# A decoder layer's last experts: four finished late, weights in megabytes, sums loaded through GpSimd's queue

## The chip, the cores and the metric

The kernel runs on one core of a Trainium2 chip. The metric is the time of one execution on the device in microseconds (us), the median of several runs. TensorE does the matrix products, VectorE and ScalarE the element-wise work, GpSimd a few small operations and the gathers and scatters by index; SyncE issues most transfers. Sixteen DMA engines move the data of all queues.

## What is computed

One decoder layer on 1024 tokens of width 1024 in float32: a chunked recurrence and a sliding-window attention, gated and mixed, then a LayerNorm, then a mixture of 32 experts (each token goes to one group of eight and there to two experts), then a second LayerNorm. Only the experts and the second LayerNorm matter here:

```python
def expert_block(args):
    xb, e = args
    h = jax.nn.silu(xb @ w_gate[e]) * (xb @ w_up[e])
    return h @ w_down[e]
...
    y = jnp.zeros((T, D), x.dtype).at[slot_tok].add(ybuf * slot_w[:, None].astype(x.dtype))
...
x = layer_norm(DN_ALPHA * x + moe, ln2_g[l], ln2_b[l])
```

An expert's weights are 1024x512 twice and 512x1024 once, 6 MB.

## The kernel before

The first tokens of an expert are gathered at 760 us; from there the experts run one after the other, in the order of `ORDER`, with the experts of `LAST` at the end. An expert's number below is its place in that order, 0 to 31. Its tokens are gathered by index on GpSimd (xg), turned by TensorE, and multiplied.

*Splits.* A float32 matrix is used as a sum of two parts: `split` casts a rounded part on ScalarE (eh, L98) and subtracts it on VectorE (el, L99), and `mm3` makes three products of the parts (L103 to L105). The weights from expert 31's gate on (and down of 30 and 31, which come later) are used unsplit, as float32 straight from the fetched tile er (L1187).

*Pieces.* `first_pieces` lists the weights in 384 pieces of 512 KB in the order of use: gate and up of expert e+1 (eight pieces), then down of e (four). `fetch` issues a piece's load on SyncE, at most DEEP = 8 under way. `moe` goes through the pieces: `halve` asks for the split of the piece LA = 3 ahead, then the steps that are due are written (results, sums), then the products of the piece, then a fetch. The order in which each engine gets its instructions here is the order in which this loop writes them.

*Results.* A normal expert's result is scaled on ScalarE and added to the sums zd in device memory by an indirect transfer of GpSimd (`accumulate`, L1090). The late experts (LAST has one of each of three groups, so no token goes to two of them) leave zd alone: their rows of zd are gathered (zf, L1086), `finish` adds the result (L1362), the LayerNorm follows in place, and the finished rows are written by index to the output (L1365). For all other tokens `final` plans the loads of zd in eight tiles z on SyncE (L1309), a sum on ScalarE (L1318), and `norm2`: mean (fm), squares on ScalarE (L1342), rsqrt (fv, on VectorE and GpSimd, L700 and L701), a gain and a shift on VectorE (L1346, L1349), and the store on SyncE (L1322). The indexed writes wait for all eight stores, since they write over some of their rows.

*Memory.* Raw pieces, both parts of a split, z, zf and scratch share 36 slots of 4 KB per partition (tag q4); a new tile waits until its slot's last user is done.

Of the kernel before, what the change touches and what calls it, by code (L numbers as in the profile page):

```python
# [23 lines left out]
LAST = (15, 23, 31)  # L24
# [37 lines left out]
class Builder:  # L62
# [5 lines left out]

    S2 = {"ob", "as", "aph", "apl", "ach", "acl", "oT", "hq", "hk", "hl", "hv", "hg", "hkd", "hkT", "hqb", "hst", "hE", "hS", "hsq", "ho",
          "rxT", "rlT", "hh", "hth", "htl"}  # L70
    NQ = 36
    NX = 9
    NRAW = 29
    LA = 3

    def __init__(self, tc, aps):
        self.tc, self.nc, self.a = tc, tc.nc, aps

    def tile(self, shape, dt, tag, bufs, name=None):
        name = name or tag  # L80
        if tag in self.S2:
            tag, bufs = "s2", self.n2
        pool = self.base if tag in ("q4", "st2", "base") else self.sb
# [78 lines left out]
    def load_x(self, half, j):  # L162
        raw = self.q4([128, 2, 512], name="xr")
        self.nc.sync.dma_start(raw, self.a["xt"][half, j])
        return raw

    def split_x(self, half, raws):

        self.xh.append([])
        self.xl.append([])  # L170
        for raw in raws:
            h, l = self.q4([128, 2, 512], F32R, "xh"), self.q4([128, 2, 512], F32R, "xl")
# [12 lines left out]
    def wload_half(self, c0, q):  # L185
        raw = self.q4([128, 4, 256], name=f"wr{c0}")
        self.nc.sync.dma_start(raw, self.a["w_in"][c0 // 256, q])
        return raw
# [4 lines left out]
    def wsplit_half(self, raw):  # L193
        h = self.q4([128, 4, 256], F32R, "wh")
        l = self.q4([128, 4, 256], F32R, "wl")
        self.split(h, l, raw)
        return h, l
# [45 lines left out]
    def att_proj(self):  # L243
# [11 lines left out]
        self.aq = [self.q4([128, 4, 256], name=f"aq{i}") for i in range(4)]  # L255
# [32 lines left out]
        self.ak = self.q4([128, T], name="ak")  # L288
# [231 lines left out]
    def hgrn(self):  # L520
# [83 lines left out]
        def prep_levels(n, hs):  # L604
            t = self.q4([128, 2, 512], F32, "hE")
# [98 lines left out]
    def mixing_loads(self):  # L704

        nc = self.nc
        self.stages, self.late_stages = {}, {}
        self.wab, self.ot, self.gates = {}, {}, {}
        wv = [self.a[nm].rearrange("(k p) c -> p k c", p=128) for nm in ("w_a", "w_b")]

        def load_wab(jt, when):
            raw = self.q4([128, 2, 4, 128], name="wab")
            for i in range(2):
                nc.sync.dma_start(raw[:, i], wv[i][:, :, jt * 128:jt * 128 + 128])
            self.at(2 * when, lambda: self.halves(self.wab, jt, raw), True)

        def load_o(b, half, nm, j):
            raw = self.q4([128, 2, 512], name=f"o{nm}")
            d = self.obd if nm == "b" else self.oad
            nc.sync.dma_start(raw, d.rearrange("k p t -> p k t")[:, 2 * j:2 * j + 2, half * 512:half * 512 + 512])  # L720
# [15 lines left out]
    def halves(self, dst, key, raw, eng=None):  # L736
        h, l = self.q4(raw.shape, F32R, "h"), self.q4(raw.shape, F32R, "l")
        self.split(h, l, raw, eng)
        dst[key] = h, l
# [23 lines left out]
    def mixing(self):  # L763
# [27 lines left out]
        def load_wo(b, p):  # L791
            raw = self.q4([128, 2, 512], name="wo")
            c, kp = p // 4, p % 4
            nc.sync.dma_start(raw, wov[:, 2 * kp:2 * kp + 2, c * 512:c * 512 + 512])
            self.at(2 * b + 2, lambda: halves(wo, p, raw, nc.gpsimd))
# [5 lines left out]
        def branch(half, jt):  # L801
# [10 lines left out]
            if jt % 2 == 0:  # L812
                mg[jt // 2] = self.q4([128, 2, 512], F32R, "mh"), self.q4([128, 2, 512], F32R, "ml")
# [71 lines left out]
        for b in range(24, 31):  # L885
            for _ in range(2 if b % 2 else 1):
                at(before, b, lambda b: self.fetch())
# [3 lines left out]
        while tick < 2 * len(main) or stages or self.late_stages:  # L891
# [19 lines left out]
            if tick >= 2 * len(main) - 1:  # L911
                for _ in range(4 if tick < 2 * len(main) + 1 else 2):
                    self.fetch(True)
# [179 lines left out]
    def first_pieces(self):  # L1093
# [14 lines left out]
        self.first_whole = self.pieces.index((NE - 1, "w_g", 0))  # L1108
        self.raws, self.fetched = {}, []

    def whole(self, e, m):

        return self.pieces.index((e, m, 0)) >= self.first_whole

    def fetch(self, first=False):

        n = len(self.fetched)
        if n >= len(self.pieces) or first and n >= self.NRAW:
            return
        e, m, k = self.pieces[n]  # L1120
        x = ORDER[e]
        if m == "w_d":
            r = self.q4([128, 1, D], name="er")
            ins = self.nc.sync.dma_start(r, self.a[m][x].rearrange("(k p) c -> p k c", p=128)[:, k:k + 1])
        else:
            r = self.q4([128, 2, 512], name="er")
            ins = self.nc.sync.dma_start(r, self.a[m][x, k])
# [115 lines left out]
    def halve(self, i):  # L1243
        if i >= len(self.pieces):
            return
        e, m, k = self.pieces[i]
        raw = self.raws.pop(i)
        if i >= self.first_whole:
            self.V["w", e, m, k] = raw, None
            return  # L1250
        h = self.q4(raw.shape, F32R, name="eh")
        l = self.q4(raw.shape, F32R, name="el")
        self.split(h, l, raw)
        self.V["w", e, m, k] = h, l

    def step(self, at, fn):

        self.steps.setdefault(int(at), []).append(fn)

    def moe(self):  # L1260
# [18 lines left out]
        self.final(at[NE - len(LAST) - 1, "w_d", 3] + 3)  # L1279
        for i in range(n):  # L1280
            self.halve(i + self.LA)
            self.now = i
            for fn in self.steps.pop(i, []):
                fn()
# [3 lines left out]
            if post:  # L1288
                self.step(i + 1 + (i < n - 4), post)
            self.fetch()  # L1290
# [6 lines left out]
    def final(self, first):  # L1297
# [9 lines left out]
        def load(i):  # L1307
            z = self.q4([128, D], name="z")
            nc.sync.dma_start(z, self.zd[i * 128:i * 128 + 128, :])  # L1309
            self.zs.append(z)  # L1310

        def rows(e):
            self.zf[e] = self.q4([128, D], name="zf")
            self.gather_rows(self.zf[e], self.zd, e)

        def sums(i):
            s = self.tile([128, 1], F32, "fs", 3)
            nc.scalar.activation(self.q4([128, D], name="w"), self.zs[i], AF.Copy, accum_out=s)  # L1318
# [6 lines left out]
        for i in range(8):  # L1325
            self.step(first + i, lambda i=i: load(i))
            self.step(first + 8 + 1.75 * i, lambda i=i: self.norm2(self.zs[i], sums(i), lambda: store(i)))
        for j in range(len(LAST)):
            self.step(first + 8 + j, lambda j=j: rows(NE - len(LAST) + j))
        self.stored = int(first + 8 + 1.75 * 7) + 4  # L1330

    def norm2(self, z, s, then):

        nc, vec = self.nc, self.nc.vector
        m, v = self.tile([128, 1], F32, "fm", 3), self.tile([128, 1], F32, "fv", 3)
# [5 lines left out]
        def square():  # L1341
            nc.scalar.activation(self.q4([128, D], name="w"), z, AF.Square, bias=m, accum_out=v)  # L1342
# [9 lines left out]
        square()  # L1352
        self.step(self.now + 1, gain)
        self.step(self.now + 2, shift)
# [47 lines left out]
    def more(self, e):  # L1402
# [16 lines left out]
        for nm in ("w_g", "w_u"):  # L1419
            ps = self.bank("mm")  # L1420
            for k in range(8):
                w = self.st2()
                nc.sync.dma_start(w, self.a[nm][bass.ds(e, 1), k // 2].rearrange("o p i c -> (o p) i c")[:, k % 2])
# [11 lines left out]
        wv = self.a["w_d"][bass.ds(e, 1)].rearrange("o (k p) c -> p (o k) c", p=128)  # L1435
        for j in range(2):
            ps = self.bank("mm")
            for k in range(4):
                w = self.st2()
                nc.sync.dma_start(w, wv[:, k, j * 512:j * 512 + 512])  # L1440
# [37 lines left out]
def gate_up(w):  # L1478

    return np.ascontiguousarray(w.reshape(NE, 4, 2, 128, 512).transpose(0, 1, 3, 2, 4))  # L1480


def arrays(inputs):
# [15 lines left out]
        "w_g": gate_up(f["w_exp_gate"][0]),  # L1499
        "w_u": gate_up(f["w_exp_up"][0]),  # L1500
        "w_d": f["w_exp_down"][0],
# [18 lines left out]
```

## Time and profile before

| | |
|---|---|
| median of 3 runs | 1399.96 us (1399.85 to 1399.97) |
| the profiled execution | 1399.95 us, its span 1398.2 us |
| TensorE busy | 1335.6 us (96%) |
| VectorE busy | 1080.5 us (77%) |
| ScalarE busy | 789.4 us (56%) |
| GpSimd busy | 241.8 us (17%) |

Busy time and span are those of the one profiled execution; 1.75 us of its time lie outside the span. In the profile's rows PE is TensorE, DVE VectorE, ACT ScalarE, POOL GpSimd, SP SyncE; a q behind the name is the engine's queue of DMA issues. Times are microseconds from the span's start, unless in ns.

### The profile page before, as it was taken

What the parts mean: (1) busy time and instruction counts of PE and PEld (TensorE: products, weight loads), DVE (VectorE), ACT (ScalarE), POOL (GpSimd) and SP (SyncE); (2) the same over time, 40 slices, a digit from 0 to 9 for tenths busy, and PEclk for the clock granted to TensorE, in tenths of its full rate; (3) what the DMA queues carried; (4) which work ended last, traced back from release to release, by engine and by line L of the source; (5) the groups of instructions that cost most, each with busy time, mean ns of one, the idle gap of its engine ahead of it and who ended that gap; (6) DMA issues with size and microseconds to landing.
All of it is one profiled execution on the core that took longest, in us unless ns stands there. A gap on an engine that the chain in (4) does not pass through costs nothing. (4 is left out here: it accounts for less than half of the span.)

```text
span 1398.2 us, 22818 instructions
## 1 busy us (share of the span) xinstructions
PE 1335.6 (96%) x8314; PEld 1100.5 (79%) x8314; DVE 1080.5 (77%) x1798; ACT 789.4 (56%) x1282; POOL 241.8 (17%) x160
## 2 busy tenths in 40 slices
PE   7999999999999999999998999999999999999844
PEld 5888899987788887788787888888888888888621
DVE  4268985779989956668656989999999999999645
ACT  4367644335545532312112888888888888888542
POOL 0001312120000002300001122222222222222123
PEclk9999999999999999999999999999999999999967
DMA  6124232153444436763557999999999999999962
GB/s 246 56 89 145 100 112 76 39 169 114 137 128 146 148 103 194 254 211 121 196 195 287 356 368 369 366 356 354 353 357 358 352 358 357 367 360 365 369 251 97
DMA packets 142564, 327.84 MB, mean 234 GB/s; under 512 B 18614, under 2 KB 59702, under 8 KB 142448
## 3 DMA queue, kind: packets, MB, share of 16 engines
q1 hardware_dynamic: 132800, 308.78, 60.9%
q0 software_dynamic: 9648, 17.57, 4.9%
q8 instruction: 66, 1.08, 0.3%
q14 instruction: 50, 0.41, 0.1%
HBM read 291.43 MB, written 52.43 MB: 246 GB/s over the span
## 5 line engine op out<-in xcount | busy, mean ns | idle before, releaser
L99 DVE TENSOR_TENSOR el<-er,eh 128x1024 fp32r<-128x1024 f32 x368 | 436.8, 1223 | 53.4 <-ACT eh L98 37.8
L98 ACT CAST eh<-er 128x1024 fp32r<-128x1024 f32 x368 | 369.7, 1054 | 99.5 <-PE mm L104 82.7
L103 PE MATMUL mm<-xh,wh 128*128 128x512 f32 x480 | 194.9, 406 | 7.8 <-ACT wh L98 6.8
L103 PE MATMUL mm<-eh,xh 128*128 128x512 f32 x496 | 196.4, 396 | 0.0
L104 PE MATMUL mm<-el,xh 128*128 128x512 f32 x496 | 196.2, 395 | 0.0
L105 PE MATMUL mm<-eh,xl 128*128 128x512 f32 x496 | 196.1, 395 | 0.0
L104 PE MATMUL mm<-xl,wh 128*128 128x512 f32 x480 | 189.0, 394 | 0.8 <-DVE xl L99 0.8
L105 PE MATMUL mm<-xh,wl 128*128 128x512 f32 x480 | 189.1, 394 | 0.0
L103 PEld LDWEIGHTS mm<-xh,wh 128*128 128x128 f32 x480 | 91.4, 190 | 25.7 <-ACT wh L98 6.8
L105 PEld LDWEIGHTS mm<-eh,xl 128*128 128x128 f32 x496 | 93.2, 188 | 22.5
L104 PEld LDWEIGHTS mm<-el,xh 128*128 128x128 f32 x496 | 93.2, 188 | 22.3
L103 PEld LDWEIGHTS mm<-eh,xh 128*128 128x128 f32 x496 | 93.2, 188 | 22.3
L105 PEld LDWEIGHTS mm<-xh,wl 128*128 128x128 f32 x480 | 91.2, 190 | 20.6 <-DVE wl L99 0.8
L1086 POOL DMA_INDIRECT xg<-x1d,gi x32 | 58.1, 1816 | 279.3 <-PE pb L1149 255.4
L104 PEld LDWEIGHTS mm<-xl,wh 128*128 128x128 f32 x480 | 91.4, 190 | 17.7 <-DVE xl L99 1.1
L103 PE MATMUL mm<-eh,hth 128*128 128x512 f32 x240 | 100.2, 418 | 0.0
L1090 POOL DMA_INDIRECT zd<-y,gi x29 | 69.8, 2407 | 156.5 <-ACT y L1240 156.5
L105 PE MATMUL mm<-eh,htl 128*128 128x512 f32 x240 | 94.8, 395 | 0.0
L104 PE MATMUL mm<-el,hth 128*128 128x512 f32 x240 | 94.8, 395 | 0.0
L103 PE MATMUL mm<-wh,xh 128*128 128x256 f32 x256 | 73.1, 286 | 0.0
L105 PE MATMUL mm<-wh,xl 128*128 128x256 f32 x256 | 72.4, 283 | 0.0
L104 PE MATMUL mm<-wl,xh 128*128 128x256 f32 x256 | 72.4, 283 | 0.0
(257 smaller groups left out, 2522.7 us busy)
## 6 DMA issues: line engine op xcount, KB each, us to landing
er<-w_g SPq DMA_DIRECT2D x128, 512.0 KB
er<-w_u SPq DMA_DIRECT2D x128, 512.0 KB
er<-w_d SPq DMA_DIRECT2D x128, 512.0 KB
wr<-w_in SPq DMA_DIRECT2D x38, 512.0 KB
gated<-st SPq DMA_DIRECT2D x32, 256.0 KB
st<-gated SPq DMA_DIRECT2D x32, 256.0 KB
xr<-xt SPq DMA_DIRECT2D x8, 512.0 KB
wab<-w_a SPq DMA_DIRECT2D x16, 256.0 KB
```

Of the source, the lines that this page charges most:

```text
L98: self.nc.scalar.copy(hi, src)
L99: (eng or self.nc.vector).tensor_sub(lo, src, hi.bitcast(F32))
L103: mm(out, lh, rh, start=start, stop=False)
L104: mm(out, lh, rl, start=False, stop=False)
L105: mm(out, ll, rh, start=False, stop=stop)
L1086: self.nc.gpsimd.indirect_dma_start(to, None, rows, bass.IndirectOffsetOnAxis(ap=self.column(self.gi, e), axis=0), bounds_check=T - 1, oob ...
L1090: self.nc.gpsimd.indirect_dma_start(self.zd, bass.IndirectOffsetOnAxis(ap=idx, axis=0), y, None, bounds_check=T - 1, oob_is_err=False, com ...
```

## The change

- Four experts are late instead of three, so 28 accumulates instead of 29, four gathers zf and four indexed writes.
- The 36 slots of 4 KB become 18 of 8 KB. A fetch loads two pieces at once, 1 MB in rows of 8 KB (the host lays the weights out so), DEEP becomes 4; the two parts of a split share a slot, and so do two z or two zf.
- The loads of z are issued by GpSimd instead of SyncE, at the steps F+3 to F+6, where F (`first`) is the last piece of expert 27; the gathers zf follow at F+7 to F+10, the sums from F+17.
- The fetches of the last eight megabytes (gate and up of 31, down of 30 and 31) are written from F+8 on.
- From F on the due steps are written ahead of `halve`, the products' own steps first. The steps of `norm2` lie further apart. Scratch moves to another pool.
- Only expert 31 is used unsplit; down of 30 is split.

```diff
-LAST = (15, 23, 31)
+LAST = (7, 15, 23, 31)
...
-    NQ = 36
+    NQ = 18
     NX = 9
-    NRAW = 29
+    NRAW = 14
     LA = 3
...
-    def q4(self, shape, dt=F32, name="q4"):
-        return self.tile(shape, dt, "q4", self.NQ, name)
+    def q8(self, shape, dt=F32, name="q8"):
+        return self.tile(shape, dt, "q8", self.NQ, name)
+
+    def q4(self, shape, pair, dt=F32):
+
+        if pair in self.pairs:
+            t = self.pairs.pop(pair)[:, 1024:2048]
+        else:
+            t = self.pairs[pair] = self.q8([128, 2048], dt, str(pair[0]))
+            t = t[:, 0:1024]
+        return self.shaped(t, shape)
...
+    def halved(self, src, eng=None):
+
+        hi, lo = self.parts(src.shape)
+        self.split(hi, lo, src, eng)
+        return hi, lo
+
+    def parts(self, shape):
+        t = self.q8([128, 2048], F32R, "hl")
+        return self.shaped(t[:, 0:1024], shape), self.shaped(t[:, 1024:2048], shape)
...
-        self.first_whole = self.pieces.index((NE - 1, "w_g", 0))
         self.raws, self.fetched = {}, []
 
     def whole(self, e, m):
 
-        return self.pieces.index((e, m, 0)) >= self.first_whole
+        return e == NE - 1
 
     def fetch(self, first=False):
 
         n = len(self.fetched)
-        if n >= len(self.pieces) or first and n >= self.NRAW:
+        if 2 * n >= len(self.pieces) or first and n >= self.NRAW:
             return
...
+        e, m, k = self.pieces[2 * n]
+        r = self.q8([128, 2, D] if m == "w_d" else [128, 4, 512], name="er")
+        ins = self.nc.sync.dma_start(r, self.a[m][ORDER[e], k // 2])
         if n >= self.DEEP:
             self.after(ins, self.fetched[n - self.DEEP])
...
-    DEEP = 8
+    DEEP = 4
...
-        h = self.q4(raw.shape, F32R, name="eh")
-        l = self.q4(raw.shape, F32R, name="el")
-        self.split(h, l, raw)
-        self.V["w", e, m, k] = h, l
...
+        raw = self.raws[i // 2]
+        n = raw.shape[1] // 2
+        raw = raw[:, n * (i % 2):n * (i % 2) + n]
+        self.V[("w",) + self.pieces[i]] = (raw, None) if self.whole(*self.pieces[i][:2]) else self.halved(raw)
...
-        self.final(at[NE - len(LAST) - 1, "w_d", 3] + 3)
+        first = at[NE - len(LAST) - 1, "w_d", 3]
+        self.late = []
+        self.final(first)
         for i in range(n):
-            self.halve(i + self.LA)
             self.now = i
-            for fn in self.steps.pop(i, []):
+            todo = [lambda: self.halve(i + self.LA)]
+            todo[i <= first and 1:0] = self.steps.pop(i, [])
+            for fn in todo:
                 fn()
             for fn in turns.pop(i, []):
                 turn(i, fn)
             post = self.piece(*self.pieces[i])
             if post:
-                self.step(i + 1 + (i < n - 4), post)
-            self.fetch()
+                self.step(i + 1 + (i < n - 4), post, i > first)
+            if i % 2:
+                for _ in range(1 if i < first + 4 else 2):
+                    if i > first + 6 or 2 * len(self.fetched) < first + 24:
+                        if len(self.fetched) + len(self.late) < (i + self.LA) // 2 + self.NQ - 1:
+                            self.fetch()
...
         def load(i):
-            z = self.q4([128, D], name="z")
-            nc.sync.dma_start(z, self.zd[i * 128:i * 128 + 128, :])
+            z = self.q4([128, D], ("z", i // 2))
+            self.late += [i] * (1 - i % 2)
+            nc.gpsimd.dma_start(z, self.zd[i * 128:i * 128 + 128, :])
             self.zs.append(z)
...
         for i in range(8):
-            self.step(first + i, lambda i=i: load(i))
-            self.step(first + 8 + 1.75 * i, lambda i=i: self.norm2(self.zs[i], sums(i), lambda: store(i)))
+            self.step(first + 3 + i // 2, lambda i=i: load(i))
+            self.step(first + 17 + 2.4 * i, lambda i=i: self.step(self.now + 1, lambda s=sums(i): self.norm2(self.zs[i], s, lambda: store(i))))
         for j in range(len(LAST)):
-            self.step(first + 8 + j, lambda j=j: rows(NE - len(LAST) + j))
-        self.stored = int(first + 8 + 1.75 * 7) + 4
+            self.step(first + 7 + j, lambda j=j: rows(NE - len(LAST) + j))
+        self.stored = int(first + 17 + 2.4 * 7) + 6
...
-        square()
-        self.step(self.now + 1, gain)
-        self.step(self.now + 2, shift)
+        for n, fn in ((1, square), (2, gain), (4, shift)):
+            self.step(self.now + n, fn)
...
-        "w_d": f["w_exp_down"][0],
+        "w_g": blocks(f["w_exp_gate"][0]),
+        "w_u": blocks(f["w_exp_up"][0]),
+        "w_d": blocks(f["w_exp_down"][0]),

```

GpSimd's instructions from the last accumulates on (xg: tokens of an expert; zd<-y: an accumulate; z: sums; zf: rows of a late expert; fv: rsqrt), before:

```order
L1090 DMA zd<-y,gi 1024x1024
L1086 DMA xg_8003<-x1d,gi 128x1024
L1090 DMA zd<-y,gi 1024x1024 x2
L1086 DMA zf<-zd,gi 128x1024 x2
L701 TENSOR_TENSOR fv<-fv,mhalf 128x1
L1086 DMA zf<-zd,gi 128x1024
L701 TENSOR_TENSOR fv<-fv,mhalf 128x1 x8
L1365 DMA out<-zf,gi 1024x1024
```

and with the change, where the last accumulate shown is that of expert 27:

```order
L1112 DMA zd<-y,gi 1024x1024
L1108 DMA xg_7832<-x1d,gi 128x1024
L1112 DMA zd<-y,gi 1024x1024
L1330 DMA z<-zd 128x1024 x8
L1108 DMA zf<-zd,gi 128x1024 x4
L725 TENSOR_TENSOR fv<-fv,mhalf 128x1 x10
L1386 DMA out<-zf,gi 1024x1024 x2
```

The eight z loads are new in this queue, between the last accumulate and the gathers.

VectorE's instructions from the last half-wide pair (xl, htl: expert 30's tokens and expert 29's hidden rows) to the first finish, before:

```order
L99 TENSOR_TENSOR htl<-pb,hth 128x512
L99 TENSOR_TENSOR el<-er,eh 128x1024 x8
L1227 TENSOR_TENSOR hh<-hh,mm 128x512
L1339 TENSOR_SCALAR fm<-fs 128x1 x2
L700 TENSOR_SCALAR fv<-fv 128x1
L1346 SCALAR_TENSOR_TENSOR z<-z,fm,ln_g 128x1024
L1349 SCALAR_TENSOR_TENSOR z<-z,fv,ln_b 128x1024
L700 TENSOR_SCALAR fv<-fv 128x1
L1346 SCALAR_TENSOR_TENSOR z<-z,fm,ln_g 128x1024
L1339 TENSOR_SCALAR fm<-fs 128x1
L1349 SCALAR_TENSOR_TENSOR z<-z,fv,ln_b 128x1024
L1362 SCALAR_TENSOR_TENSOR zf,fs_14062<-mm,tw,zf 128x512 x2
```

and with the change:

```order
L117 TENSOR_TENSOR hl<-er,hl 128x1024 x2
L117 TENSOR_TENSOR htl<-pb,hth 128x512
L117 TENSOR_TENSOR hl<-er,hl 128x1024
L1383 SCALAR_TENSOR_TENSOR zf,fs_13002<-mm,tw,zf 128x512 x2
L1359 TENSOR_SCALAR fm<-fs_13002 128x1
L117 TENSOR_TENSOR hl<-er,hl 128x1024 x2
L724 TENSOR_SCALAR fv<-fv 128x1
L1368 SCALAR_TENSOR_TENSOR zf<-zf,fm,ln_g 128x1024
L117 TENSOR_TENSOR hl<-er,hl 128x1024 x2
L1371 SCALAR_TENSOR_TENSOR zf<-zf,fv,ln_b 128x1024
L1361 TENSOR_SCALAR fm<-fs 128x1
L117 TENSOR_TENSOR hl<-er,hl 128x1024 x2
```

The finish of expert 28 (two rows, zf) stands ahead of the last eight splits (hl), and the steps of z and zf stand between these.

ScalarE's instructions at the same place (eh, hl: casts of splits; y: a result scaled; hh: silu; w: sums and squares), before:

```order
L98 CAST eh<-er 128x1024
L1240 ACTIVATE y<-mm,tw 128x512 x2
L98 CAST eh<-er 128x1024 x4
L1223 ACTIVATE hh<-mm 128x512
L98 CAST eh<-er 128x1024 x3
L1318 ACTIVATE w,fs<-z 128x1024
L1342 ACTIVATE w,fv<-z,fm 128x1024
L1158 COPY xh<-pb 128x512 x2
L1318 ACTIVATE w,fs<-z 128x1024
L1342 ACTIVATE w,fv<-z,fm 128x1024
```

and with the change:

```order
L116 CAST hl<-er 128x1024 x2
L116 CAST hth<-pb 128x512
L116 CAST hl<-er 128x1024 x2
L1364 ACTIVATE w,fv<-zf,fm 128x1024
L116 CAST hl<-er 128x1024 x2
L1340 ACTIVATE w,fs<-z 128x1024
L116 CAST hl<-er 128x1024
L1239 ACTIVATE hh<-mm 128x512
L116 CAST hl<-er 128x1024
L1340 ACTIVATE w,fs<-z 128x1024
L1364 ACTIVATE w,fv<-z,fm 128x1024
L116 CAST hl<-er 128x1024 x2
```

The square over zf (L1364) stands between the casts of F+17 and F+18, and sums and squares over z (L1340, L1364) between the later ones; before, they stood behind all casts.

## Rows read from the trace of the kernel before

**Rows 1.** The view by stretches, while experts run and in the stop.
```profile
core 0: us, PE busy (x) PEld busy (x) DVE busy (x) ACT busy (x) POOL busy (x), PEclk, DMA share, GB/s
1253.11:1271.22 18.11, 18.11 (x86) 14.76 (x85) 16.39 (x17) 14.81 (x19) 4.36 (x2) 1.00 1.01 359
1320.00:1330.00 10.00, 3.01 (x16) 2.12 (x14) 0.00 (x0) 0.00 (x0) 0.86 (x1) 0.86 0.98 377
1330.00:1340.00 10.00, 0.00 (x0) 0.00 (x0) 0.00 (x0) 0.00 (x0) 0.00 (x0) 0.50 0.96 352
```

**Rows 2.** The list of waits: two lines.
```profile
PE mm L1187 <- ACT xh L1158: 23.0, 1, 23.0
ACT w L1318 <- DMA z<-zd: 25.6, 1, 25.6
```

**Rows 3.** TensorE's timeline, 1310 to 1346 (start, us, ...).
```profile
1310.11 0.40 PE L105 MATMUL mm<-eh,xl 128*128 128x512 f32 x1
1310.34 0.40 PE L103 MATMUL mm<-eh,xh 128*128 128x512 f32 x1
...
1322.62 0.40 PE L105 MATMUL mm<-eh,htl 128*128 128x512 f32 x1
1345.97 16.55 PE L1187 MATMUL mm<-er,xh 128*128 128x512 f32 x32 [22.96 <-ACT xh L1158]
```

**Rows 4.** SyncE's timeline (start, time to issue them, ...).
```profile
1298.78 4.45 SPq L1124 DMA_DIRECT2D er<-w_d  x4
1304.17 4.14 SPq L1127 DMA_DIRECT2D er<-w_g  x4
...
1317.40 11.78 SPq L1124 DMA_DIRECT2D er<-w_d  x8
...
1332.61 9.19 SPq L1309 DMA_DIRECT2D z<-zd  x8
```

**Rows 5.** GpSimd's timeline, gathers and an accumulate.
```profile
1282.43 1.90 POOL L1086 DMA_INDIRECT xg<-x1d,gi  x1 [8.74 <-PE pb L1149]
1289.33 2.47 POOL L1090 DMA_INDIRECT zd<-y,gi  x1 [5.00 <-ACT y L1240]
...
1319.82 1.04 POOL L1086 DMA_INDIRECT zf<-zd,gi  x1 [0.40 <-PE mm L105]
```

**Rows 6.** DMA issues over the whole span: accumulates, us from issue to landing.
```profile
zd<-y,gi POOLq DMA_INDIRECT x29, 9.9
```

**Rows 7.** DMA by queue, 1286 to 1287: GpSimd's queue, share of 16 engines.
```profile
q0 software_dynamic: 4, 0.02, 4.8%
```

**Rows 8.** DMA by queue, 1287 to 1288: all, SyncE's queue, GpSimd's queue.
```profile
DMA packets 101, 0.39 MB, mean 393 GB/s; under 512 B 5, under 2 KB 5, under 8 KB 101
q1 hardware_dynamic: 62, 0.23, 58.3%
q0 software_dynamic: 39, 0.16, 39.3%
```

**Rows 9.** DMA by queue, 1295 to 1296: GpSimd's queue.
```profile
q0 software_dynamic: 39, 0.12, 60.0%
```

**Rows 10.** Groups by line and shape, from 1280 to the end.
```profile
L99 DVE TENSOR_TENSOR el<-er,eh 128x1024 fp32r<-128x1024 f32 x25 | 29.7, 1223 | 4.9 <-ACT eh L98 4.2 <-PE pb L1149 0.3 <-PE mm L104 0.3
L98 ACT CAST eh<-er 128x1024 fp32r<-128x1024 f32 x25 | 25.5, 1055 | 9.0 <-PE mm L104 6.2 <-PE mm L105 2.5
...
L1349 DVE SCALAR_TENSOR_TENSOR z<-z,fv,ln_b 128x1024 f32<-128x1024 f32 x8 | 10.3, 1284 | 2.9 <-POOL fv L701 2.4 <-DMA z<-zd 0.5
L1346 DVE SCALAR_TENSOR_TENSOR z<-z,fm,ln_g 128x1024 f32<-128x1024 f32 x8 | 10.2, 1276 | 0.0
...
L1362 DVE SCALAR_TENSOR_TENSOR zf<-mm,tw,zf 128x512 f32<-128x512 f32 x6 | 4.3, 746 | 0.0
```

**Rows 11.** VectorE's timeline: last shift of z, last shift of all.
```profile
1376.01 1.29 DVE L1349 SCALAR_TENSOR_TENSOR z<-z,fv,ln_b 128x1024 f32<-128x1024 f32 x1 [0.44 <-POOL fv L701]
...
1389.20 1.28 DVE L1349 SCALAR_TENSOR_TENSOR zf<-zf,fv,ln_b 128x1024 f32<-128x1024 f32 x1 [0.46 <-POOL fv L701]
```

**Rows 12.** GpSimd's timeline: a write of finished rows.
```profile
1385.79 1.04 POOL L1365 DMA_INDIRECT out<-zf,gi  x1 [2.68 <-DVE zf L1362]
```

More of the change, by code (lines that the diff above doesn't have):

```diff
@@ L77, in __init__ @@
         self.tc, self.nc, self.a = tc, tc.nc, aps
+        self.pairs = {}
     def tile(self, shape, dt, tag, bufs, name=None):
@@ L86, in tile, with shaped @@
         return pool.tile(list(shape), dt, name=name, tag=tag, bufs=bufs)
-    def q4(self, shape, dt=F32, name="q4"):
-        return self.tile(shape, dt, "q4", self.NQ, name)
+    def q8(self, shape, dt=F32, name="q8"):
[7 more added lines that the diff above has]
+        return self.shaped(t, shape)
+    @staticmethod
+    def shaped(t, shape):
+        if len(shape) == 2:
+            return t
+        names = "abc"[:len(shape) - 1]
+        return t.rearrange("p (%s) -> p %s" % (" ".join(names), " ".join(names)), **{n: k for n, k in zip(names, shape[1:])})
     def st2(self, shape=(128, 512)):
@@ L162, in load_x @@
     def load_x(self, half, j):
-        raw = self.q4([128, 2, 512], name="xr")
+        raw = self.q4([128, 2, 512], ("xr", half, j // 2))
         self.nc.sync.dma_start(raw, self.a["xt"][half, j])
@@ L193, in wsplit_half @@
     def wsplit_half(self, raw):
[L194 to L197, printed above, removed]
+        return self.halved(raw)
     def proj_T(self, w, ct, half):
@@ L254, in att_proj @@
         raw3 = self.wload(2560)
-        self.aq = [self.q4([128, 4, 256], name=f"aq{i}") for i in range(4)]
+        self.aq = [self.q4([128, 4, 256], ("aq", i // 2)) for i in range(4)]
         def keep(ps, ch, ct, half):
@@ L736, in halves @@
     def halves(self, dst, key, raw, eng=None):
-        h, l = self.q4(raw.shape, F32R, "h"), self.q4(raw.shape, F32R, "l")
-        self.split(h, l, raw, eng)
-        dst[key] = h, l
+        dst[key] = self.halved(raw, eng)
     def mixing_start(self):
@@ L812, in branch @@
             if jt % 2 == 0:
-                mg[jt // 2] = self.q4([128, 2, 512], F32R, "mh"), self.q4([128, 2, 512], F32R, "ml")
+                mg[jt // 2] = self.parts([128, 2, 512])
             def post():
@@ L885, in mixing @@
         for b in range(24, 31):
-            for _ in range(2 if b % 2 else 1):
+            if b != 27:
                 at(before, b, lambda b: self.fetch())
@@ L911, in mixing @@
             if tick >= 2 * len(main) - 1:
-                for _ in range(4 if tick < 2 * len(main) + 1 else 2):
+                for _ in range(2 if tick < 2 * len(main) + 1 else 1):
                     self.fetch(True)
@@ L1245, in halve, with step @@
             return
[L1246 to L1250, printed above, removed]
-        h = self.q4(raw.shape, F32R, name="eh")
-        l = self.q4(raw.shape, F32R, name="el")
-        self.split(h, l, raw)
-        self.V["w", e, m, k] = h, l
-    def step(self, at, fn):
-        self.steps.setdefault(int(at), []).append(fn)
+        raw = self.raws[i // 2]
+        n = raw.shape[1] // 2
+        raw = raw[:, n * (i % 2):n * (i % 2) + n]
+        self.V[("w",) + self.pieces[i]] = (raw, None) if self.whole(*self.pieces[i][:2]) else self.halved(raw)
+    def step(self, at, fn, urgent=False):
+        fns = self.steps.setdefault(int(at), [])
+        fns.insert(0 if urgent else len(fns), fn)
     def moe(self):
@@ L1307, in load @@
         def load(i):
[L1308 to L1309 removed]
+            z = self.q4([128, D], ("z", i // 2))
+            self.late += [i] * (1 - i % 2)
+            nc.gpsimd.dma_start(z, self.zd[i * 128:i * 128 + 128, :])
             self.zs.append(z)
         def rows(e):
[L1313 removed]
+            self.zf[e] = self.q4([128, D], ("zf", e // 2))
+            self.late += [e] * (1 - e % 2)
             self.gather_rows(self.zf[e], self.zd, e)
@@ L1439, in more @@
                 w = self.st2()
-                nc.sync.dma_start(w, wv[:, k, j * 512:j * 512 + 512])
+                wv = self.a["w_d"][bass.ds(e, 1), k // 2].rearrange("o p i c -> (o p) i c")
+                nc.sync.dma_start(w, wv[:, k % 2, j * 512:j * 512 + 512])
                 nc.tensor.matmul(ps, hT[:, k], w, start=k == 0, stop=k == 3)
```

46 lines of the change are left out of this document (18 added, 28 removed).

## The prediction

> **What bounds the kernel now.** I read the view by stretches first. While the experts run, TensorE is busy for the whole of a stretch, VectorE for nine tenths of it, and the DMA engines are full [rows 1]. Nothing that is only off TensorE's path can gain there. The same view shows where TensorE stands: it works 3 of the 10 us from 1320 and none of the 10 us from 1330, at a granted clock that has fallen to 0.50, its lower level. The list of waits names the reason in two lines: TensorE waited 23.0 us for ScalarE's copy of the last tokens (xh), and ScalarE waited 25.6 us for the first rows of the sums, z [rows 2]. ScalarE works in order, and the sum over z stood ahead of that copy. In TensorE's own rows the stop lies between 1323.0 and 1345.97 [rows 3]. The reader is to see in SyncE's rows why z was late: its loads stand behind all weights and are issued from 1332.61 [rows 4]. So the change goes for a stop of 23 us. It pays if the work after it comes earlier and no new wait takes its place.
>
> I count pieces from F, the last piece of expert 27 (in order of work). Gate and up of 29 are F+1 to F+8, down of 28 F+9 to F+12, gate and up of 30 F+13 to F+20, down of 29 F+21 to F+24; then expert 31. TensorE ends F+16 at 1310.5 [rows 3].
>
> **What is moved, and what waits now.** The eight z loads go to GpSimd's queue behind the accumulate of expert 27, and zf of expert 28 is gathered behind them. On VectorE the finish of expert 28, which waits for this zf, now stands ahead of the split of F+17 (second order listing). VectorE works in order, so with that split TensorE's F+17 waits too, and behind it the whole rest. The question is when this zf lands. I call the moment Z.
>
> The accumulate of 27 starts at 1289.33 [rows 5] and accumulates land 9.9 us after their issue [rows 6]: the first z load can start at 1299.2. A gather issued at 1282.43 [rows 5] puts its first packets on the engines in the last part of the microsecond from 1286 [rows 7], 4.4 us later; taken for z, the data starts at 1303.6. In front of zf are 8 x 0.52 MB, with zf itself 4.7 MB. All 16 engines move 0.39 MB per us [rows 8]. How much of that GpSimd's queue gets while weights are queued no row of z tells, since z was alone at the end. The nearest rows are a gather, with 39% of the engines in a full microsecond [rows 8], and an accumulate, with 60% in its best one [rows 9]. I take half, because z is eight whole loads in a row, where the gather's microsecond holds parts of single rows: 4.7 MB at 0.195 MB per us are 24 us, and **Z is 1327.5**. At 60% it is 1323.7, at 39% 1334.5, with the engines alone 1315.7. It can't be much later than 1340: before, the same bytes kept the engines full until the last z, issued at 1341.8 [rows 4] and landed some 4 us later, and only three other gathers and half of the last expert's down weights (2 MB at 0.39, 5 us) may come after this zf. GpSimd's own issue doesn't bind: eight at 1.04 to 2.47 us [rows 5] are 8 to 20 us, under the 24.
>
> The Trainium skill has a rule against this part ("DMA: Bandwidth & Descriptors", section "Issuing engines are not separate DMA queues"): transfers started by GpSimd or SyncE run on the same 16 DMA engines and interleave, so another issuing engine saves issue time alone. The trace agrees: the hardware queue's share falls to 58% while the other has 39% [rows 8]. By this rule z wins only its place ahead of the held weights; without it one would set the engines-alone value of Z, 12 us earlier.
>
> The weights are held back in the program, but hardly in time: the first held one now waits for the fourth megabyte before it, and without any holding it was issued at 1304.17 [rows 4], after z's new start. So they compete, and I price the holding at nothing.
>
> **From Z to the end, by VectorE's order.** Finish of 28: two halves at 0.75 [rows 10] and a mean, 1.6. Then the splits of F+17 to F+24, which no longer run three ahead. There are 18 double slots: z has four, zf two, weights not yet split ten (w_u of 30 and w_d of 29 two each, of the held eight the first six). Two are left for split pairs; so the cast of F+18 waits for TensorE's end of F+17. A pair of pieces then costs a split (1.22), six products at 0.233 less what ran before (together 1.4, from the pitch of [rows 3]), a cast (1.05), a split (1.22) and a step of a result between them (1.28) [rows 10]: 6.2. This holds for the first two pairs; then slots come free and a pair costs 2 splits, one cast and one step, 4.8. The last split ends at Z + 1.6 + 12.4 + 9.6 = Z + 23.6. Up to the last shift of z there follow 17 steps at 1.28, four splits of expert 30's down weights (4.9, new: they were used unsplit), three operations of half a split's width (1.8), two finishes (3.0), 31.5 in all, and waits for rsqrt, before 2.9 over eight z [rows 10]: Z + 58.0. TensorE keeps up under this: unsplit gate and up of expert 31 took 16.55 [rows 3], the new 24 products of d(30) take 5.6, all beside VectorE's 34.4.
>
> From the end of the last shift of z (1377.3) to the end of VectorE's last one (1390.5) before took 13.2 [rows 11]: store, writes of finished rows, rsqrt behind these on GpSimd, last result. The fourth late expert adds one write there, 1.04 [rows 12]: 14.2. Then 7.7 to the span's end, as before (1398.2 - 1390.5), and 1.75 around the span. Sum: Z + 58.0 + 14.2 + 7.7 + 1.75 = Z + 81.7 = **1409.2**, against 1399.95 of the profiled execution, which is the median of the runs (1399.96) to 0.01.
>
> The rest I price at nothing. One accumulate fewer goes from GpSimd, idle there. The 1 MB fetches halve SyncE's issues, which bind nothing while TensorE runs without a wait; faster or slower, they change the lead of the weights, still 12 pieces at 1304.17 (F+25 is issued, and TensorE, four pieces of 1.4 before 1310.5, begins F+13) [rows 3, 4], so weights later by some 10 us would be hidden. Past that each microsecond would show. The paired slots of the early stages may shift some waits; TensorE's order there is unchanged, and I allow 2 us either way. A slower clock after the new stop, as in [rows 1], may cost some 3 us.
>
> **Rivals.**
> - **GpSimd's loads starve.** The held weights are in longer rows now; if they take over 61% of the engines, Z is 1334.5 to 1340 and the time 1416 to 1422. For it: the 39%. Against: the 60%.
> - **Faster.** Splits stay three ahead because slots come free early enough (the earlier weights may be gone sooner than I count), and the first z have the engines nearly alone because weights are held. A pair then costs 2 x 1.22 + 1.28 = 3.7; four save 2 x 2.5 + 2 x 1.1 = 7.2, and with Z from 1315.7 to 1322 the time is 1390.2 to 1396.5. It decides when Z is 1322 or less with a free slot for every split. For it: the program asks for splits three pieces ahead (LA), and TensorE never waited for one before 1323. Against: ten weights plus six sums in 18 slots.
> - **One of these two alone.** The engines alone, but slots short: 1397.4 to 1403.7; slots free at half the engines: 1402.
> - **The change doesn't do what it says**, in that nothing is held in time; this is inside the forecast already.
>
> **Numbers.** 0.2% is 2.8 us, about what a measurement here can tell from no change: faster is under 1397.2, slower over 1402.8. The forecast with shares from 39% to 60% (1405.4 to 1416.2) has 0.50, the starved case 0.15, the faster rival 0.17, one of the two alone 0.18. From these: slower 0.50 + 0.15 and little of the last; the last is mostly no change, with a few hundredths below it, where clock or early stages help. So 0.22 faster, 0.14 same, 0.64 slower. The range leaves out the top of the starved case and the bottom of the faster one: 1394 to 1419.
>
> **What would show it.** Right: TensorE's wait at 1323 is gone, and a new one of some 15 us stands at F+17 from about 1312, whose releaser is VectorE's split, and VectorE's wait is for zf; z's landing is spread over 1307 to 1325 with GpSimd's queue at about half the engines; pairs of casts wait for TensorE; VectorE's last shift is near 1400. Wrong: zf lands before VectorE asks for it, at about 1312, or VectorE's last shift comes before 1388; then Z or the slots were mispriced. If TensorE waits before 1300 for weights, the fetches are.

## The result and the profile after

The change is slower: 1420.28 us, the median of four runs (1420.08 to 1421.43), against 1399.97 of before (four runs, 1399.85 to 1401.11). The ratio is 1.0145, with a 95% interval of 1.0127 to 1.0163. The forecast was 1409 with a range of 1394 to 1419: right in the sign, 11 us short in the size, and the time lies just outside the range. The profiled execution took 1420.47 us with a span of 1418.7, 20.5 us more than before.

The list of waits of the changed kernel shows the old stop gone and another in its place. The columns are: engine, line, what waited for what, us in total, times, longest.

```profile
PE mm L132 <- DVE hl L117: 30.4, 9, 25.2
ACT w L1364 <- DVE fm L1359: 32.2, 4, 24.7
DVE zf L1383 <- DMA zf<-zd,gi: 24.1, 1, 24.1
```

Of the two lines of [rows 2] only TensorE's wait for xh is still in the list, with 0.7 us. Read the three from the bottom: VectorE waited 24.1 us for the gathered rows zf of expert 28; ScalarE waited 24.7 us for the mean (fm) that the same finish makes; TensorE waited 25.2 us for VectorE's split. Before, TensorE stood for 23.0 us. So TensorE's stop was replaced by one that is 2.2 us longer, and it comes earlier in the order of the work, with the splits of F+17 to F+24 behind it.

The view by stretches shows what the stop looks like. Beside the rows of [rows 1] for 1320 to 1340, TensorE's stop starts earlier, and the DMA engines move more.

```profile
core 0: us, PE busy (x) PEld busy (x) DVE busy (x) ACT busy (x) POOL busy (x), PEclk, DMA share, GB/s
1310.00:1320.00 10.00, 2.17 (x7) 1.23 (x7) 1.23 (x1) 1.67 (x2) 3.93 (x4) 0.89 1.02 419
1320.00:1330.00 10.00, 0.00 (x0) 0.00 (x0) 0.00 (x0) 0.00 (x0) 0.00 (x0) 0.50 1.02 419
1330.00:1340.00 10.00, 1.15 (x3) 0.96 (x4) 2.78 (x6) 1.24 (x2) 0.00 (x0) 0.50 0.82 328
```

From 1320 to 1330 nothing computes at all, the granted clock is at its lower level, and 4.19 MB move (419 GB/s). The core was waiting for data while it moved more of them per us than in any stretch of [rows 1] (at most 377), so the question is whose data they were.

GpSimd's timeline shows the order in its queue, and SyncE's what came against it (start, time to issue, what). The gather that VectorE waits for is the first of the four zf, issued at 1309.87; it landed at Z, 26.1 us later.

```profile
1287.82 2.21 POOL L1112 DMA_INDIRECT zd<-y,gi  x1 [4.13 <-ACT y L1256]
1299.72 4.33 POOL L1330 DMA_DIRECT2D z<-zd  x8 [9.69 <-DVE hl L117]
1309.87 1.08 POOL L1108 DMA_INDIRECT zf<-zd,gi  x1 [5.82 <-issue]
```
```profile
1296.45 4.04 SPq L1143 DMA_DIRECT2D er<-w_d  x2
...
1302.63 3.93 SPq L1143 DMA_DIRECT2D er<-w_g  x2
1310.02 4.08 SPq L1143 DMA_DIRECT2D er<-w_u  x2
1322.62 23.98 SPq L1143 DMA_DIRECT2D er<-w_d  x4
```

The z loads were issued at 1299.72, half a microsecond from the forecast's 1299.2. The "held" weights were issued from 1302.63, 1.5 us earlier than without any holding ([rows 4]: 1304.17). The landings, from the DMA issues of 1285 to the end (size, median us from issue to landing), give the price:

```profile
z<-zd POOLq DMA_DIRECT2D x8, 512.0 KB, 18.2
...
zf<-zd,gi POOLq DMA_INDIRECT x4, 27.3
```

How the 16 engines were shared is in the view of DMA by queue (packets, MB, share of 16 engines). First 1308 to 1310, then 1320 to 1322; q1 is SyncE's queue, q0 GpSimd's.

```profile
q1 hardware_dynamic: 106, 0.43, 51.9%
q0 software_dynamic: 109, 0.40, 48.8%
...
q1 hardware_dynamic: 74, 0.57, 69.1%
q0 software_dynamic: 73, 0.27, 33.0%
```

In both stretches the two queues had equally many packets but for a few, 106 to 109 and 74 to 73; in 2-us stretches from 1312 to 1330 GpSimd's share is 32 to 40%. The bytes differ. In the first stretch shown, SyncE's packets are 4 KB (0.43 MB by 106; the gain and the bias of the LayerNorm were being loaded there), and the engines are shared by halves. In the second they are some 8 KB, rows of the 1 MB fetches, against 4 KB rows of z: SyncE's queue gets two thirds and GpSimd's one third. In the last 6 us before Z, as the gathers come, GpSimd's packets are shorter (0.50 MB by 396, 305 of all packets under 512 B), and its share is 24%.

VectorE's timeline then gives the way from Z to the end. Z, the landing of zf, is where the first row stands.

```profile
1335.98 0.75 DVE L1383 SCALAR_TENSOR_TENSOR zf<-mm,tw,zf 128x512 f32<-128x512 f32 x1 [24.10 <-DMA zf<-zd,gi]
...
1337.58 1.22 DVE L117 TENSOR_TENSOR hl<-er,hl 128x1024 fp32r<-128x1024 f32 x1
1342.46 1.22 DVE L117 TENSOR_TENSOR hl<-er,hl 128x1024 fp32r<-128x1024 f32 x1 [3.67 <-ACT hl L116]
...
1349.88 1.23 DVE L117 TENSOR_TENSOR hl<-er,hl 128x1024 fp32r<-128x1024 f32 x1 [3.81 <-ACT hl L116]
...
1360.14 1.23 DVE L117 TENSOR_TENSOR hl<-er,hl 128x1024 fp32r<-128x1024 f32 x1 [1.11 <-ACT hl L116]
...
1393.98 1.28 DVE L1371 SCALAR_TENSOR_TENSOR z<-z,fv,ln_b 128x1024 f32<-128x1024 f32 x1
...
1408.26 1.28 DVE L1371 SCALAR_TENSOR_TENSOR zf<-zf,fv,ln_b 128x1024 f32<-128x1024 f32 x1 [1.55 <-POOL fv L725]
```

Against [rows 11]: the last shift of z ends at 1395.26 instead of 1377.3 (18.0 us later), VectorE's last operation at 1409.54 instead of 1390.48 (19.1 later), and the span 20.5 later. So 18 of the 20.5 us are in place before the tail begins.

### The profile page after: what moved, and what is told of

Read it like the earlier page. It is cut to its first block, busy times and chain, and to the rows that moved or that the text cites. A ratio compares the mean times of both kernels' runs of the same rounds, so it can differ in the third digit from the quotient of the medians.

```text
span 1418.7 us, 22074 instructions
## 1 busy us (share of the span) xinstructions
PE 1339.5 (94%) x8322; PEld 1103.0 (78%) x8322; DVE 1091.9 (77%) x1811; ACT 794.3 (56%) x1286; POOL 237.0 (17%) x170
## 3 DMA queue, kind: packets, MB, share of 16 engines
q8 instruction: 66, 1.08, 0.3%
## 5 line engine op out<-in xcount | busy, mean ns | idle before, releaser
L117 DVE TENSOR_TENSOR hl<-er,hl 128x1024 fp32r<-128x1024 f32 x372 | 441.3, 1221 | 66.6 <-ACT hl L116 64.4
L116 ACT CAST hl<-er 128x1024 fp32r<-128x1024 f32 x372 | 376.9, 1055 | 109.2 <-PE mm L133 103.6
L131 PE MATMUL mm<-hl 128*128 128x512 f32 (+1 forms) x992 | 369.6, 373 | 8.9 <-ACT hl L116 8.2
L133 PE MATMUL mm<-hl 128*128 128x512 f32 (+1 forms) x992 | 361.3, 364 | 2.6 <-DVE hl L117 2.6
L132 PE MATMUL mm<-hl 128*128 128x512 f32 (+1 forms) x992 | 360.4, 363 | 0.8 <-DVE hl L117 0.8
L132 PE MATMUL mm<-hl,xh 128*128 128x512 f32 x496 | 198.4, 400 | 28.0 <-DVE hl L117 28.0
L131 PEld LDWEIGHTS mm<-hl 128*128 128x128 f32 x992 | 187.6, 189 | 38.6 <-ACT hl L116 9.5
L133 PEld LDWEIGHTS mm<-hl 128*128 128x128 f32 x992 | 187.4, 189 | 36.3 <-DVE hl L117 6.5
L132 PEld LDWEIGHTS mm<-hl 128*128 128x128 f32 x992 | 187.8, 189 | 27.3 <-DVE hl L117 1.3
L131 PE MATMUL mm<-hl,xh 128*128 128x512 f32 x496 | 198.0, 399 | 3.4 <-ACT hl L116 3.4
L133 PE MATMUL mm<-hl,xl 128*128 128x512 f32 x496 | 197.7, 399 | 0.0
L132 PEld LDWEIGHTS mm<-hl,xh 128*128 128x128 f32 x496 | 93.9, 189 | 52.3 <-DVE hl L117 30.2
L131 PEld LDWEIGHTS mm<-hl,xh 128*128 128x128 f32 x496 | 93.9, 189 | 27.8 <-ACT hl L116 5.4
L133 PEld LDWEIGHTS mm<-hl,xl 128*128 128x128 f32 x496 | 94.2, 190 | 22.4
L131 PE MATMUL mm<-hl,hth 128*128 128x512 f32 x248 | 104.9, 423 | 0.0
L132 PE MATMUL mm<-hl,hth 128*128 128x512 f32 x248 | 99.2, 400 | 1.6 <-DVE hl L117 1.6
L133 PE MATMUL mm<-hl,htl 128*128 128x512 f32 x248 | 98.7, 398 | 0.0
L405 POOL TENSOR_TENSOR aph<-aph,const 128x512 fp32r<-128x512 f32 x14 | 24.1, 1722 | 242.9 <-DVE anm L381 113.2
```

Source lines behind the costliest of these rows:

```text
L131: mm(out, lh, rh, start=start, stop=False)
L132: mm(out, lh, rl, start=False, stop=False)
L133: mm(out, ll, rh, start=False, stop=stop)
L405: nc.gpsimd.tensor_mul(p, p.bitcast(F32), gt)
```

## The experiments

Two theories on the size of Z were put against each other. **A**: the DMA engines take the packets of the two queues by turns, so the share goes by the length of a row, and 8 KB weight rows leave z a third. **B**: GpSimd's queue is slow by itself, whatever runs beside it. All edits below are edits of the changed kernel. Experiments 1 to 4 and 6 are one run each. The first four ran beside one run of the kernel before (1400.31), the last three beside seven (median 1399.12, 1398.44 to 1400.13).

### 1. The same weights in rows of 4 KB

```diff
-        ins = self.nc.sync.dma_start(r, self.a[m][ORDER[e], k // 2])
...
+        parts = [slice(0, cut), slice(cut, 2 * cut)] if 2 * n >= len(self.pieces) - 28 else [slice(0, 2 * cut)]
+        for part in parts:
+            ins = self.nc.sync.dma_start(r[:, part], src[:, part])
```

The last 14 MB of weights are fetched as two transfers of 512 KB each; slots, steps and bytes stay.

> The last 28 pieces are fetched in rows of 4 KB (two transfers of 512 KB for each megabyte), all else as in the change. Z is the landing of zf of expert 28 (1335.9 in the change). Theory A, the DMA engines take one packet from each queue by turns, so the length of the rows sets the shares: both queues have rows of 4 KB, GpSimd's share goes from 34% to 45 to 50%, Z to 1326 to 1329, the time to 1410 to 1414. Theory B, GpSimd's queue is held to about 0.14 MB per us by itself: share, Z and time as in the change (1336, 1420).

Measured: 1410.07 us, 10.2 less than the change. DMA by queue, first from 1308 to 1310 and then from 1322 to 1326, and four rows of VectorE's timeline:

```profile
q0 software_dynamic: 117, 0.43, 52.7%
q1 hardware_dynamic: 116, 0.42, 51.2%
...
q1 hardware_dynamic: 329, 1.20, 76.3%
q0 software_dynamic: 331, 0.38, 27.1%
```
```profile
1326.84 0.75 DVE L1387 SCALAR_TENSOR_TENSOR zf<-mm,tw,zf 128x512 f32<-128x512 f32 x1 [15.07 <-DMA zf<-zd,gi]
...
1349.89 1.23 DVE L117 TENSOR_TENSOR hl<-er,hl 128x1024 fp32r<-128x1024 f32 x1 [1.12 <-ACT hl L116]
...
1383.73 1.28 DVE L1375 SCALAR_TENSOR_TENSOR z<-z,fv,ln_b 128x1024 f32<-128x1024 f32 x1
...
1397.86 1.28 DVE L1375 SCALAR_TENSOR_TENSOR zf<-zf,fv,ln_b 128x1024 f32<-128x1024 f32 x1 [1.55 <-POOL fv L725]
```

The queues still have equal packets, 117 to 116, and now the bytes are equal too. Z comes at 1326.84, 9.1 earlier. The edit halves the row and, with it, the transfer (512 KB instead of 1 MB), so the time alone doesn't part the two; the packets do. From 1322 to 1326 SyncE's transfers are the same, GpSimd's packets are shorter (274 of all 660 under 512 B), the counts are equal again, 329 to 331, and the bytes are 1.20 to 0.38 MB. That fits A, and B, by which share and Z would have stayed, falls.

### 2. The last eight megabytes really held

```diff
+        if 2 * n >= len(self.pieces) - 16:
+            self.after(ins, self.zlast)
```

`zlast` is the last load of z.

> The last eight megabytes of weights wait for the landing of the last z: they are held back in time, not only in the program. Theory A: z has the engines nearly alone from 1304, Z is 1315 to 1319, the time 1399 to 1404. Theory B: Z stays above 1328, the time above 1412.

Measured: 1409.47 us, 5.5 us above the expectation of A. DMA by queue from 1306 to 1308, then GpSimd's queue from 1314 to 1318 and from 1318 to 1322, both queues from 1322 to 1326, then VectorE:

```profile
q1 hardware_dynamic: 76, 0.57, 67.8%
q0 software_dynamic: 70, 0.27, 32.4%
```
```profile
q0 software_dynamic: 429, 1.56, 98.0%
...
q0 software_dynamic: 620, 1.13, 78.9%
...
q1 hardware_dynamic: 33, 0.27, 27.0%
q0 software_dynamic: 99, 0.32, 19.6%
```
```profile
1324.94 0.75 DVE L1385 SCALAR_TENSOR_TENSOR zf<-mm,tw,zf 128x512 f32<-128x512 f32 x1 [12.76 <-DMA zf<-zd,gi]
```

Once the weights ahead of the held ones were through, GpSimd's queue had the engines alone and moved 1.56 MB in 4 us, 0.39 MB per us: a second time against B. The expectation was missed for two reasons. What is not held, the down weights of expert 29 in rows of 8 KB and then the gain and the bias, still brought 2.6 MB through SyncE's queue from 1302 to 1314 (0.90, 1.01 and 0.70 MB in three stretches of 4 us), with two thirds of the engines at 1307, packet for packet with z. Holding back what comes later does nothing to what is already in the queue. And once the gathers came, GpSimd's queue no longer filled engines that stood free: it took 79% from 1318 to 1322 and 20% from 1322 to 1326, where SyncE's had 27%, while VectorE waited until 1324.94. So a part of Z is no matter of sharing; why is open. The held weights were issued at 1323.71, and no engine waited for them after that; the end is Z + 84.5, as without the hold (Z here 1324.9, the time 1409.47; in the change 1336.0 and 1420.47).

### 3. Two more slots for splits

```diff
-                        if len(self.fetched) + len(self.late) < (i + self.LA) // 2 + self.NQ - 1:
+                        if len(self.fetched) + len(self.late) < (i + self.LA) // 2 + self.NQ - (1 if i < first else 3):
```

From F on two slots fewer hold weights, so four are left for split pairs.

> The late fetches leave two more of the 18 slots to split pairs (four instead of two); the order of work stays. If the lack of slots costs what the prediction's sum says, the last split (F+24) ends some 17 us after Z instead of 25, and with the same Z or one up to 3 us earlier the time is 1410 to 1416. If it costs nothing, the distance from Z to the end stays 84 and the time is 1417 to 1420.

Measured: 1411.90 us, 8.4 less than the change. VectorE's timeline:

```profile
1334.56 0.75 DVE L1383 SCALAR_TENSOR_TENSOR zf<-mm,tw,zf 128x512 f32<-128x512 f32 x1 [26.30 <-DMA zf<-zd,gi]
...
1338.48 1.23 DVE L117 TENSOR_TENSOR hl<-er,hl 128x1024 fp32r<-128x1024 f32 x1 [1.11 <-ACT hl L116]
...
1351.54 1.23 DVE L117 TENSOR_TENSOR hl<-er,hl 128x1024 fp32r<-128x1024 f32 x1 [1.11 <-ACT hl L116]
```

The second split waits 1.11 us, the length of a cast, and not 3.67 for a cast that had itself waited for TensorE. The last split ends at 1352.77 = Z + 18.2, against Z + 25.4 in the change: the shortage of slots cost 7.2 us once the stop was over. The stop itself stays (26.30).

### 4. The z loads back to SyncE, at the change's place

```diff
-            nc.gpsimd.dma_start(z, self.zd[i * 128:i * 128 + 128, :])
+            nc.sync.dma_start(z, self.zd[i * 128:i * 128 + 128, :])
```

The loads are still written at F+3 to F+6, ahead of the last fetches; only the queue is another.

> The z loads are issued by SyncE again, at the change's place in the program, so in one queue ahead of the held weights. Theory A: one queue has no turns to take, z goes before the held weights and has all engines but for one gather: Z is 1316 to 1321, the time 1400 to 1406. If GpSimd's queue is what brings z early, Z is later than 1336 and the time over 1420.

Measured: 1393.09 us, 27.2 less than the change and 7.2 less than the kernel before beside it (one run each). GpSimd's, SyncE's and VectorE's timelines, a row of each:

```profile
1299.83 1.96 POOL L1108 DMA_INDIRECT zf<-zd,gi  x1 [10.06 <-issue]
```
```profile
1300.82 15.72 SPq L1330 DMA_DIRECT2D z<-zd  x8
```
```profile
1311.53 0.74 DVE L1383 SCALAR_TENSOR_TENSOR zf<-mm,tw,zf 128x512 f32<-128x512 f32 x1
```

The finish of expert 28 has no wait at all: the gather is issued at 1299.83 with nothing ahead of it in its queue, and is there when VectorE comes to it. The time is 7 us under the expectation, which had not counted that zf now waits for nothing in its queue. Z is out of the sum here. But this run changes two things: z is in another queue, and zf no longer stands behind z. Experiment 6 parts them.

### 5. Experiments 3 and 4 together

Both edits above.

> z on SyncE (as in e4_sync) and four slots for split pairs (as in e3_slots) together. Theory: the two costs stand behind one another on VectorE's path, so they add up: 1393.1 less the 7 us that the slots gave in e3_slots, 1385 to 1388. Rival: with z out of the way the slots bind no longer, or TensorE or the weights bind instead: 1391 to 1394.

Measured: 1391.21 us, median of four (1389.50 to 1393.83), ratio to before 0.9939 (0.9922 to 0.9955). It is faster than before, but 3 us above what the theory expected and in the rival's range of 1391 to 1394, and the gain over experiment 4 is too small to be told from none. The profiled execution is the slowest of the four, 1393.83. Two rows of its SyncE timeline, one of VectorE's and one of ScalarE's:

```profile
1300.10 3.73 SPq L1143 DMA_DIRECT2D er<-w_d  x2
...
1304.90 16.57 SPq L1330 DMA_DIRECT2D z<-zd  x8
```
```profile
1319.32 1.28 DVE L1368 SCALAR_TENSOR_TENSOR zf<-zf,fm,ln_g 128x1024 f32<-128x1024 f32 x1 [2.51 <-DMA ln_g<-ln_g]
```
```profile
1322.41 1.06 ACT L1340 ACTIVATE w<-z 128x1024 f32<-128x1024 f32 x1 [5.99 <-DMA z<-zd]
```

The fetch of w_d is issued at 1300.10, in experiment 4 at 1295.05, and on SyncE everything behind it is later too: ln_g, ln_b, and the z loads at 1304.90 instead of 1300.82. The first splits no longer wait for slots, and ScalarE waits 5.99 us for z instead. The last split starts at 1334.06, in experiment 4 at 1333.40. So the trace goes with the rival in this: with the wait for zf gone, something else binds, here z itself. Why SyncE is late is open, and the slots are not shown to be the reason: in experiment 3, with the same slots, w_d was issued at 1296.39, and SyncE's fetches were late here by 2.6 us at 1240.03 already (1237.43 in experiment 4), long before F, where the edit starts to count.

### 6. All on GpSimd's queue, zf ahead of z

```diff
-            self.step(first + 3 + i // 2, lambda i=i: load(i))
+            self.step(first + 5 + i // 2, lambda i=i: load(i))
...
-            self.step(first + 7 + j, lambda j=j: rows(NE - len(LAST) + j))
+            self.step(first + 3 + j // 2, lambda j=j: rows(NE - len(LAST) + j))
```

> z stays on GpSimd's queue, but the four gathers zf are issued ahead of the eight z instead of behind them; two slots for split pairs as in the change. Theory: the price of the change is that zf stands behind 4.2 MB in its own queue; then zf lands by 1311, VectorE waits for nothing at finish 28, z lands in time for the sums, and the time is 1392 to 1398, near e4_sync. Rival: GpSimd's queue as such is the price, since z and the gathers share a third of the engines: zf lands in time, but z late, ScalarE's sums wait and hold the casts, and the time is 1403 to 1412.

Measured: 1396.84 us, 23.4 less than the change, in the range that the theory expected. GpSimd, VectorE and ScalarE:

```profile
1301.55 1.04 POOL L1108 DMA_INDIRECT zf<-zd,gi  x1 [9.96 <-DVE hh L1243]
...
1307.13 2.22 POOL L1330 DMA_DIRECT2D z<-zd  x4
```
```profile
1313.37 0.75 DVE L1383 SCALAR_TENSOR_TENSOR zf<-mm,tw,zf 128x512 f32<-128x512 f32 x1
```
```profile
1322.31 1.06 ACT L1340 ACTIVATE w<-z 128x1024 f32<-128x1024 f32 x1 [1.24 <-DMA z<-zd]
```

The same eight loads in the same queue, against the same 8 KB rows, cost little once the small gather goes first: VectorE's wait is gone, and the sum over z waits 1.24 us. Against the kernel before beside each, the change stands at +20.3, experiment 4 at -7.2 and this one at -2.3 us. So some 23 of the 27 us between the change and experiment 4 belong to the order in GpSimd's queue, not to the queue as such.

### 7. Experiment 5 with the down weights of expert 30 unsplit again

```diff
-        return e == NE - 1
+        return e == NE - 1 or (e, m) == (NE - 2, "w_d")
```

> As e5_sync_slots, and down of expert 30 is used unsplit, as before the change: four casts, four splits and one half-wide split fewer, 16 slower products instead of 24. If VectorE's order sets the end, 5 us less than e5_sync_slots: 1380 to 1383. If TensorE has become the bound there, the same as e5_sync_slots to 2 us more.

Measured: 1389.86 us, median of four (1389.48 to 1390.15), ratio to before 0.9934 (0.9917 to 0.9950). That is 1.35 us under experiment 5, whose runs reach down to 1389.50: no difference that these runs can tell. What the four splits (4.9 us of VectorE in the forecast) are worth is open: between the two profiled executions (1393.83 and 1389.48) the way from the end of the split of F+24 to that of the last shift of z is 33.9 us in experiment 5 and 30.2 here, but the runs of experiment 5 alone lie 4.3 us apart. It is the lowest median of the versions tried, 9.3 us under the kernel before and 30 under the change.

## Why the prediction was right and wrong

The forecast's sum, by its own terms. Experiment 1 stands beside the change, as it differs from it in the length of a row and the transfers that go with it. The second line is a part of the third.

| | forecast | the change | experiment 1 |
|---|---|---|---|
| Z | 1327.5 | 1336.0 | 1326.8 |
| Z to the end of the last split | 23.6 | 25.4 | 24.3 |
| Z to the end of the last shift of z | 58.0 | 59.3 | 58.2 |
| from there to the end of VectorE's last operation | 14.2 | 14.3 | 14.1 |
| from there to the span's end | 7.7 | 9.2 | 9.2 |
| around the span | 1.75 | 1.77 | 1.77 |
| time | 1409.2 | 1420.5 | 1410.1 |

**Right: the mechanism.** TensorE's wait at 1323 is gone, a new one stands at F+17, its releaser is VectorE's split, and VectorE waits for zf, as the forecast said that a right one would show; only the wait was to be some 15 us, and is 25.2. The direction follows from that, and experiments 4 and 6 take the wait away and the loss with it. The two slots for split pairs are right too: 7.2 us by experiment 3, where the forecast's rival had 7.2 for free slots.

**Wrong: one term, the share of the engines that sets Z.** The forecast chose half of the engines, "because z is eight whole loads in a row". Z came 8.5 us later, out of 11 us missed. The share was 33% in 1320 to 1322, and experiment 1 shows why: the queues have equal packets, and a weight's packet had become twice as long as one of z. With equal rows, the queue does get about half while z is loaded, Z is 1326.8, and the forecast's 1409.2 comes within 0.9 us of the 1410.07 measured. That is in part luck. Half came from the packets, not from z being whole loads; in experiment 1 the engines moved 0.41 MB per us (1310 to 1322) and not 0.39, and the gathers at the end had 27% and not half (1322 to 1326); and a Z that is 0.7 us early makes up for a part of the tail that is 1.5 us long. The change's own diff held this: the rows of a fetch go from 4 KB to 8 KB. The forecast saw it and put it into a rival with a chance of 0.15, against the 60% of [rows 9]. That row was misread: 60% is a share of the engines' time, and its bytes are 0.12 MB in that microsecond, 31% of the 0.39 that the sum divides. It was the wrong neighbour as well, and so were [rows 8], where the packets can be divided out: 0.23 MB by 62 and 0.16 by 39 are both some 4 KB. No row of before could say what 8 KB against 4 KB does, and half was chosen as if the rows stayed equal.

The starved rival said 1416 to 1422 with Z at 1334.5 to 1340, and that is what happened: Z 1336.0 and 1420.3. It deserved most of the chance.

**Smaller misses.** From Z to the last shift 1.3 us: the granted clock was at its lower level, 0.50, when the splits began, and a pair took 7.3 and 7.4 us (starts at 1337.58, 1344.86 and 1352.29) instead of 6.2, which had been worked out from rows at the full clock. In experiment 1, after a stop 9 us shorter, the first pair took 7.3 at 0.50 as well, the second 6.3, with the clock back at 0.92 over 1336 to 1342. In experiment 4, without the stop, the first took 6.2 (1313.12 to 1319.33) at 1.00. So the two pairs took 2.3 us more than forecast, which goes with the clock; some 3 us for it stood beside the forecast's sum, without a working. The tail is 9.2 instead of 7.7: GpSimd's last write starts 1.03 us after VectorE's last operation instead of 0.29, and the span ends 8.1 after its start instead of 7.4. From VectorE's last operation to the span's end it was 8.5 to 9.2 in all seven experiments, with four late experts in each. Why is open.

**The rule that was weighed** held in part. The Trainium skill ("DMA: Bandwidth & Descriptors", section "Issuing engines are not separate DMA queues") says that another issuing engine saves issue time alone; the runs agree that the two queues share the same engines. But experiments 1, 4 and 6 show two more things that the queue decides: whose packets alternate with whose, and what stands ahead of a small gather. The section "Queues, rings and completion order" of the same page of the Trainium skill says that an engine goes round its queues packet by packet; the equal counts, 74 to 73 and 117 to 116, agree. It has a packet hold some 9 to 17 descriptors, where each packet that the profile counts here held about one row (0.57 MB by 74 and 0.27 by 73); the measurement decides. By that rule of the Trainium skill, with packets of 8 and 4 KB, an estimate of the share is a third. A third of 0.39 MB per us gives, by the forecast's own sum, an estimate of 1339.8 for Z (1303.6 and 36.2 us for 4.7 MB), 3.8 us late where half was 8.5 early.

**Priced at nothing, rightly:** the holding of the weights (issued at 1302.63, and so not later than the 1304.17 of [rows 4]) and the early stages: the accumulate of 27 starts at 1287.82, 1.5 us earlier than in [rows 5].

Not tried: three late experts with the rest of the change, and the order of steps ahead of splits by itself. So what each of these two gives or takes stays open; together with the z loads on SyncE they are inside the 7 us by which experiment 4 beats the kernel before.

## What to carry to other kernels

Before a transfer is moved to another queue, write down what stands ahead of the smallest transfer in that queue that somebody waits for: here one gather behind eight loads cost some 23 us, and ahead of them VectorE didn't wait for it. In these runs two queues that were both full had equal numbers of packets, so the bytes went by the length of a row; a fetch in longer rows took its share from the other queue. And a step that waits for data is better not written ahead of splits on the same engine, unless the data is known to be there; this rests on the waits of the change, not on an experiment of its own.

## What the runs showed of the hardware that was not expected

- While both queues were full, they had equal numbers of packets in stretches of 2 us but for a few (106 and 109, 74 and 73, 117 and 116, 76 and 70), whatever the packets' length, and with it a share of 52 to 49 or of 69 to 33. It is no rule without exception: in the last 4 us before Z in the change, with the gathers' short packets, they had 84 and 245, then 93 and 58.
- Engines that are shown as full did not always move the same: 359 GB/s while the experts ran, with the weights coming through SyncE's queue [rows 1]; 410 in the stretch of experiment 2 where z was nearly alone in GpSimd's; 419 with both (1310 to 1330 of the change). It is not the queue: SyncE's alone moved 426 in experiment 2 from 1330 to 1334 (weights in rows of 8 KB) and 414 in the kernel before from 1340 to 1344 (z in rows of 4 KB). What slows the experts' stretch is open.
- GpSimd started eight plain loads in 4.33 us, 0.54 each, where the indexed gathers of zf took 0.99 to 1.08 (up to 1.96 in experiment 4), that of xg 1.85 and an accumulate 2.21.
